# Short convolution and attention of a hybrid layer: two stages behind a barrier rewritten as one interleaved stage with other functions and another attention tail

## Chip, cores, metric

One Trainium2 chip, all 8 cores (two dies, cores 0 to 3 and 4 to 7), each with its own part of the tokens. The time is that of the slowest core in microseconds (us) of the device. A program on all cores has a slow state in some executions, in which one die shows a lower granted clock; only fast runs are compared unless the text says otherwise. Engines: PE multiplies matrices, DVE is the vector engine, ACT the scalar engine, POOL the GpSimd engine, SP issues transfers.

## The reference, cut to what matters

Two trunk layers. Each projects the input once, and two mixers read the result: grouped-query attention, and a gated delta scan whose inputs first go through a short convolution of width 3 with Silu and a norm per head. The two mixers do not depend on one another until their outputs are merged.

```python
def l2norm(x):
    xf = x.astype(jnp.float32)
    return xf * lax.rsqrt(jnp.sum(xf * xf, axis=-1, keepdims=True) + EPS)

def short_conv(x, w):                       # 1536 channels, width 3
    ...
    for j in range(1, CONV_W):
        y = y + xp[:, j:j + T] * w[j]
    return jax.nn.silu(y)

def block_attention(q, k, v):               # blocks of 128 queries, softmax in float32
    ...
        s = jnp.einsum('bkgqd,bkjd->bkgqj', qblk, k).astype(jnp.float32) * scale
        p = jax.nn.softmax(s, axis=-1).astype(v.dtype)
        return jnp.einsum('bkgqj,bkjd->bkgqd', p, v)

# in trunk_layer:
    qkv_d = short_conv(jnp.concatenate([q_d, k_d, v_d], axis=-1), conv_w)
    q_d = l2norm(q_d ...) * (DK ** -0.5);  k_d = l2norm(k_d ...)
    ...
    o_a = block_attention(q_use ..., k_all, v_all)
    o_f, S_f = delta_chunked(q_d, k_d, v_d, ...)     # and the same backwards
```

## The kernel before

Everything is recorded by small helpers (`mm`, `act`, `tt`, `stt`, `cp`, `recip`, `dma`), each with the list of what it reads and what it writes; the program derives its semaphores from these names. All matmuls therefore show one line number in the profile, all activations another, and the tile names tell them apart. Stage B, the convolution, works on blocks of 256 tokens (20 a core and layer), and a barrier (`P.fence()`) stands between it and the attention.

```python
for c in range(12):                                   # 12 x 3 DVE instructions of 128x256
    tsc("dve", CV[:, c, :], PRET[:, c, 0:TB], cw[:, 0, c:c + 1], ...)
    stt("dve", CV[:, c, :], PRET[:, c, 1:TB + 1], ...)
    stt("dve", CV[:, c, :], PRET[:, c, 2:TB + 2], ...)
for c in range(12):
    act(CV[:, c, :], CV[:, c, :], AF.Silu, ...)
for c in range(8):                                    # norms of q and k
    act(STB[0][:, :TB], CV[:, c, :], AF.Square, ...)
    mm(psb(0)[:, :TB], C("blk", True), STB[0][:, :TB], ...)
    act(STG[0][:, :TB], psb(0)[:, :TB], AF.Sqrt, ...)
    recip(STG[0][:, :TB], STG[0][:, :TB], ...)        # DVE
    stt("dve", CV[:, c, :], CV[:, c, :], ..., STG[0][:, :TB], ...)
    cp("act", STB[i][:, :TB], CV[:, c, :], ...)
    dma("pool", dstT..., STB[i][:, :TB], [f"stb{i}"], [("qkdt", s.name)])
# ... six groups of four f32 transposes, a copy and a transfer each
P.fence()
```

The attention runs over "items": one key tile of 128 against one block of 128 queries of 8 heads. The QK matmuls of item n+1 are recorded before the AV matmuls of item n (`LAG = 1`), with two score and two probability buffers. A block of the long sequence has 34 items, and ends with this tail:

```python
    for g in range(2): mm(PS[r_]..., KT_all..., QBz[qp][g], ...)      # QK of item idx
    act(XBW[r_], PS[r_], AF.Exp, ..., scale=0.125)                    # 128x1024
    for g in range(2): mm(psb(4 + g), VAp[:, kt, g, :], XBW[r_]...)   # AV of item idx - 1
    if last:
        for g in range(2):
            cp("dve", RS[64:65, :], psb(ob)[64:65, :], ...)           # the row of sums
            recip(RS[64:65, :], RS[64:65, :], ...)
            mm(psb(6)[0:64, :], C("ones")[64:65, 0:64], RS[64:65, :], ...)
            cp("dve", STG[0][0:64, :], psb(ob)[0:64, :], ...)
            tt("dve", OB, STG[0][0:64, :], psb(6)[0:64, :], ALU.mult, ...)
            dma("sp", OA..., OB..., ...)
```

## Time and profile before

| | before |
|---|---|
| time, median of 16 runs | 23658.64 us (23517.87 to 23765.41; the first four, which the prediction had, 23707.53) |
| stage B plus attention, per layer, by core | 3213 to 3265 us, mean 3235 |
| everything else of the span, by core | 17032 to 17233 us |
| loads of ACT's function tables in these stages, layer 0 | 41 |

The stage is measured on each core from the first load of the convolution's input (or of the context, if earlier) to the scan's first state load. The prediction shows the busy times and the costliest groups. For comparison with the same view after the change, here is the view of waits for the attention of layer 0 on core 4, the slowest core (columns: engine, output tile and line of what waited, what released it, then us in total, times, longest):

```profile
ACT sb_xbw L484 <- PE ps L478: 802.3, 591, 14.5
PE ps L478 <- DVE sb_bigB L505: 372.6, 80, 5.5
```

Such a wait is named after the last link of the chain, not after its cause: the first row contains the second, PE's own wait for the reciprocal of one row (line 505).

### The profile page before, as it was taken

The page shows a single profiled execution, that of the slowest core. Times are in us where ns is not written, and L with a number is a line of the kernel's source. Part 1 is how long each engine was busy: PE and PEld are TensorE (multiplying, and loading weights), DVE is VectorE, ACT ScalarE, POOL GpSimd, SP SyncE. Part 2 cuts the span into 40 slices and gives each one's busy share as a digit, 9 for nine tenths or more (in the row PEclk, how much of TensorE's full clock was granted, in tenths as well). Part 3 has the DMA queues.
Part 4 walks back from the last instruction along what each step waited for, and adds up shares of the span by engine and source line. Part 5 has one row for each costly group of instructions (what it writes and reads, how often), then busy time and mean ns, then how long its engine had stood idle before and what let it go on. Part 6 is the DMA issues. An engine that isn't in the chain of part 4 may idle for free.

```text
span 23694.1 us, 384038 instructions; the slowest of 8 cores (23508.7 to 23694.1 us)
## 1 busy us (share of the span) xinstructions
PE 12329.6 (52%) x116476; PEld 7884.9 (33%) x116700; DVE 8493.7 (36%) x13539; ACT 6954.8 (29%) x11204; POOL 4030.9 (17%) x5166
## 2 busy tenths in 40 slices
PE   2555115775655544574655521477566555349255
PEld 1333101222443333463533310122244333237144
DVE  0222452214666543220122245321365665322022
ACT  0444235663222221111134432466322222112011
POOL 1112110001333321110111211000033333111011
PEclk9777557886666667676777755687766666668577
DMA  5111110000011113311311111000011111332111
GB/s 122 47 46 44 46 48 14 5 5 18 28 29 30 30 38 91 89 67 47 85 55 47 46 44 48 22 5 5 13 28 29 30 27 29 84 95 77 28 41 39
DMA packets 1051188, 1018.80 MB, mean 43 GB/s; under 512 B 427456, under 2 KB 921024, under 8 KB 1038400
## 3 DMA queue, kind: packets, MB, share of 16 engines
q1 hardware_dynamic: 920576, 621.68, 9.2%
q0 software_dynamic: 128576, 372.53, 5.8%
q8 instruction: 967, 15.84, 0.3%
q14 instruction: 1069, 8.76, 0.1%
HBM read 688.84 MB, written 392.23 MB: 46 GB/s over the span
## 4 chain that ended last, share of the span: by engine, by line
PE 35%; DVE 18%; DMA 15%; ACT 13%; issue 13%; POOL 3%; POOLq 1%; ACTq 1%; SPq 0%; DVEq 0%
PE ps L478 34%; ACT sb_xbw L484 4%; DVE sb_stg L505 3%; DVE sb_bigB L487 3%; DMA gates_s<-sb_stb 3%; DVE sb_bigB L496 2%; DVE sb_bigB L505 2%; ACT L484 2%; DMA sb_warena<-w 2%; DMA pre_s<-sb_stg 1%; PE ps L481 1%; ACT sb_stb L484 1%; DVE sb_warena L487 1%; ACT sb_stg L484 1%; POOLq L184 1%
## 5 line engine op out<-in xcount | busy, mean ns | idle before, releaser
L478 PE MATMUL ps<-sb_hb,sb_warena 128*128 128x256 bf16 x18080 | 2538.2, 307 | 2207.2 <-DMA sb_warena<-w 1144.0
L478 PEld LDWEIGHTS ps<-sb_hb,sb_warena 128*128 128x128 bf16 x18080 | 1961.4, 110 | 2713.0 <-issue 2287.0
L484 ACT ACTIVATE sb_xbw<-ps 128x1024 bf16<-128x1024 f32 x2208 | 2199.1, 1023 | 1637.3 <-PE ps L478 1611.1
L478 PE MATMUL ps<-sb_gatb,sb_warena 128*128 128x256 bf16 (+1 forms) x18080 | 2164.6, 289 | 215.5 <-POOL sb_gatb L487 138.5
L478 PEld LDWEIGHTS ps<-sb_gatb,sb_warena 128*128 128x128 bf16 (+1 forms) x18080 | 1765.0, 111 | 589.4 <-issue 265.0
L478 PE MATMUL ps<-sb_xbw,sb_warena 128*128 128x512 bf16 x4326 | 1402.0, 406 | 374.4 <-ACT sb_xbw L484 346.7
L505 DVE RECIPROCAL sb_stg<-sb_stg 128x256 f32<-128x256 f32 x520 | 911.3, 1752 | 1765.0 <-ACT sb_stg L484 1765.0
L484 ACT ACTIVATE sb_stg<-ps,sb_b1f 128x256 f32<-128x256 f32 x1280 | 603.0, 474 | 3047.2 <-PE ps L478 2871.8
L478 PE MATMUL ps<-sb_warena,sb_kt_all 128*128 128x512 bf16 x4322 | 1419.7, 411 | 105.1 <-DMA sb_warena<-qa_p 72.8
L478 PE MATMUL ps<-sb_warena 64*64 64x64 bf16 (+1 forms) x25600 | 1113.8, 228 | 612.4 <-DMA sb_warena<-od_s 147.3
L478 PE MATMUL ps<-sb_stb,sb_cstb 128*128 128x256 bf16 x520 | 177.3, 341 | 2375.4 <-ACT sb_stb L484 2119.2
L502 DVE COPY sb_bigB<-ps 1x512 f32<-1x512 f32 (+1 forms) x180 | 134.7, 749 | 3013.7 <-PE ps L478 2747.1
L484 ACT ACT_TABLE_LOAD x745 | 955.8, 1283 | 698.0 <-PE ps L478 322.1
L478 PEld LDWEIGHTS ps<-sb_warena 64*64 64x64 bf16 (+1 forms) x25600 | 898.4, 129 | 782.6 <-issue 705.9
L487 POOL TENSOR_TENSOR sb_bigA<-sb_cst,sb_sm 128x512 f32<-128x512 f32 x160 | 163.3, 1042 | 5444.9 <-DMA sb_ktc<-kdt_s 3881.3
L487 DVE TENSOR_TENSOR sb_gatb<-sb_stg 128x256 bf16<-128x256 f32 x640 | 272.2, 425 | 2248.0 <-ACT sb_stg L484 2033.4
L487 POOL TENSOR_TENSOR sb_hb<-sb_hb,sb_cstb 128x512 bf16<-128x512 bf16 x560 | 659.2, 1195 | 1686.6 <-DVE sb_hb L487 1285.7
L478 PEld LDWEIGHTS ps<-sb_stb,sb_cstb 128*128 128x128 bf16 x520 | 52.6, 101 | 2514.7 <-issue 2514.6
L478 PEld LDWEIGHTS ps<-sb_xbw,sb_warena 128*128 128x128 bf16 x4416 | 311.0, 99 | 1366.5 <-issue 1356.2
L481 PE MATMUL ps<-sb_cst,sb_bigB 128*128 128x128 f32 x1440 | 372.3, 421 | 710.0 <-DVE sb_bigB L487 585.9
L487 DVE TENSOR_TENSOR sb_bigB<-sb_bigB,ps 64x512 f32<-64x512 f32 x640 | 436.9, 683 | 813.4 <-ACT sb_bigB L500 633.9
L478 PEld LDWEIGHTS ps<-sb_warena,sb_kt_all 128*128 128x128 bf16 x4416 | 442.2, 102 | 807.3 <-issue 425.7
(233 smaller groups left out, 21222.3 us busy)
## 6 DMA issues: line engine op xcount, KB each, us to landing
sb_bigA<-xres_s SPq DMA_DIRECT2D x64, 1024.0 KB, 5.9
sb_bigA<-pre_s SPq DMA_DIRECT2D x32, 1548.0 KB, 7.6
sb_bigB<-xres_s SPq DMA_DIRECT2D x48, 1024.0 KB, 6.0
pre_s<-sb_stg POOLq DMA_DIRECT2D x384, 128.0 KB, 2.1
gates_s<-sb_stb POOLq DMA_DIRECT2D x512, 64.0 KB, 1.8
sb_hb<-h_s SPq DMA_DIRECT2D x64, 512.0 KB, 4.2
sb_warena<-w_mod POOLq DMA_DIRECT2D x32, 768.0 KB, 6.9
xres_s<-sb_bigA POOLq DMA_DIRECT2D x24, 1024.0 KB, 5.3
```

The source lines that it names most:

```text
L184: eng.wait_ge(prod.sig_sem, prod.sig_val)
L478: P.add("pe", lambda e: e.matmul(out, lhsT, rhs, start=start, stop=stop, **kw), reads, writes)
L481: P.add("pe", lambda e: e.transpose(out, in_, ident), reads, writes)
L484: P.add("act", lambda e: e.activation(out, in_, func, **kw), reads, writes)
L487: P.add(eng, lambda e: e.tensor_tensor(out, in0, in1, op), reads, writes)
L496: P.add(eng, lambda e: e.scalar_tensor_tensor(out, in0, scalar, in1, op0, op1), reads, writes)
L502: P.add(eng, lambda e: e.tensor_copy(out, in_), reads, writes)
L505: P.add("dve", lambda e: e.reciprocal(out, in_), reads, writes)
```

## The change

The intent is to let ACT and PE work on attention items while DVE convolves, and to take DVE's reciprocals and ACT's table switches off the path. Both stages become generators; Silu and the inverse square root are written with exp and ln alone; the tail copies its accumulators out of PSUM at once and is finished during the next items. The diff, cut (the convolution loop and the transposes keep their instructions, apart from one PSUM bank, `psb(7)`, and all copies on DVE):

```diff
-                for c in range(12):
-                    act(CV[:, c, :], CV[:, c, :], AF.Silu, [("cv", c)], [("cv", c)])
+                    for c4 in range(3):
+                        SG = PRET[:, cs_, 0:TB]                  # over the convolution's input
+                        act(SG, CV[:, cs_, :], AF.Exp, ck + ["bigA"], ["bigA"], scale=-1.0)
+                        act(SG, SG, AF.Ln, ["bigA"], ["bigA"], bias=1.0)
+                        act(SG, SG, AF.Exp, ["bigA"], ["bigA"], scale=-1.0)
+                        tt("dve", CV[:, cs_, :], CV[:, cs_, :], SG, ALU.mult, ck + ["bigA"], ck)
+                        yield
-                    act(STG[0][:, :TB], psb(0)[:, :TB], AF.Sqrt, [pk(0)], ["stg0"], bias=EPS, scale=1.0)
-                    recip(STG[0][:, :TB], STG[0][:, :TB], ["stg0"], ["stg0"])
+                        act(STG[1][:, :], psb(7)[:, :], AF.Ln, [pk(7)], ["stg1"], bias=EPS, scale=1.0)
+                        act(STG[1][:, :], STG[1][:, :], AF.Exp, ["stg1"], ["stg1"], scale=-0.5)
 ... two channels at a time; the bf16 result is copied back by POOL; yield after each
-        P.fence()
 ...
+        def tail(s, q0):
+            for g in range(2):
+                cp("dve", RS2[64:65, g * 512:(g + 1) * 512], psb(4 + g)[64:65, :], [pk(4 + g)], ["rs"])
+                cp("dve", NUM[g][0:64, :], psb(4 + g)[0:64, :], [pk(4 + g)], [("num", g), f"stg{2 * g}"])
+            def inv():
+                act(RS2[64:65, :], RS2[64:65, :], AF.Ln, ["rs"], ["rs"])
+                act(RI[64:65, :], RS2[64:65, :], AF.Exp, ["rs"], ["ri"], scale=-1.0)
+            def out(g): ...        # one-row matmul in bf16, DVE product, transfer
+            return [inv, lambda: out(0), lambda: out(1)]
 ...
+                    if last:
+                        for fn in pend: fn()
+                        pend[:] = tail(s, q0)
+                    elif pend:
+                        pend.pop(0)()
 ...
+        gB_, gAt_ = genB(), genAttn()
+        while not (doneB and doneA):
+            ... next(gB_)                                        # one piece of stage B
+            for _ in range(3 + (1 if it_ % 4 == 3 else 0)):
+                ... next(gAt_)                                   # then 3.25 items on average
+            it_ += 1
```

## The prediction

> **What bounds the kernel now.** I first read the clocks of the cores: spans of 23509 to 23694 us, both dies alike, so one core (core 4, the slowest) stands for all. Then I looked for the two stages that the change touches, the short convolution ("B") and the attention, by the first transfer of each: the loads of the convolution's input begin at 2456.1 us, those of the attention's queries at 3742.5, and the scan's first state load is at 5668.9; in layer 1 the same marks are 13812, 15092 and 17060. The table of busy time in these four stretches of core 4 (columns: stretch and its length, busy us of PE, weight loads, DVE, ACT and POOL with counts, granted clock, DMA share, GB/s):
> ```profile
> 2456.00:3742.00 1286.00, 181.59 (x642) 107.83 (x642) 680.29 (x1083) 373.83 (x840) 161.84 (x281) 0.50 0.14 46
> 3742.00:5669.00 1927.00, 1298.54 (x4484) 393.42 (x4576) 431.82 (x321) 1089.96 (x1105) 4.81 (x1) 0.84 0.03 6
> 13812.00:15092.00 1280.00, 181.32 (x641) 107.60 (x641) 672.62 (x1082) 373.64 (x840) 153.86 (x281) 0.50 0.14 46
> 15092.00:17060.00 1968.00, 1369.60 (x4485) 404.34 (x4577) 439.79 (x323) 1111.72 (x1105) 12.68 (x2) 0.79 0.03 6
> ```
> The reader is to see two stages of opposite kind, one after the other behind a barrier. B is 53% DVE, 29% ACT and nearly no PE; the attention is PE and ACT with DVE idle. Together 3213 us in layer 0 and 3248 in layer 1: 6461 of 23694 us. No engine is full in either, so both are bound by waits. The groups by form say which, for B:
> ```profile
> L505 DVE RECIPROCAL sb_stg<-sb_stg 128x256 f32<-128x256 f32 x160 | 280.4, 1753 | 422.8 <-ACT sb_stg L484 422.8
> L496 DVE SCALAR_TENSOR_TENSOR sb_bigB<-sb_bigA,sb_cw,sb_bigB 128x256 f32<-128x256 f32 x480 | 232.5, 484 | 51.2 <-DVE sb_bigB L491 0.9
> L484 ACT ACT_TABLE_LOAD x40 | 51.3, 1283 | 32.5 <-DVE sb_bigB L496 19.8 <-PE ps L478 11.9 <-DVE sb_bigB L491 0.8
> ```
> and for the attention:
> ```profile
> L484 ACT ACTIVATE sb_xbw<-ps 128x1024 bf16<-128x1024 f32 x1103 | 1087.7, 1022 | 799.4 <-PE ps L478 788.5 <-ACT sb_xbw L484 1.6
> L505 DVE RECIPROCAL sb_bigB<-sb_bigB 1x512 f32<-1x512 f32 x77 | 257.5, 3344 | 8.6 <-DVE sb_bigB L502 0.9
> L478 PE MATMUL ps<-sb_bigB,sb_cst 1*64 1x512 f32 x152 | 146.0, 1061 | 354.3 <-DVE sb_bigB L505 354.3
> ```
> In B each of 160 normalisations goes round ACT, PE, ACT, DVE: the reciprocal alone is 1.753 us and DVE waits another 2.6 (422.8/160) for ACT. In the attention ACT waits 799 us for PE; half of that (354 us) is PE waiting for the 3.3 us reciprocal of a single row at the end of every query block. The order of time inside a query block shows the rest:
> ```profile
> 4306.37 1.94 ACT L484 ACTIVATE sb_xbw<-ps 128x1024 bf16<-128x1024 f32 x2 [0.40 <-PE ps L478]
> 4308.72 1.02 ACT L484 ACTIVATE sb_xbw<-ps 128x1024 bf16<-128x1024 f32 x1 [0.41 <-PE ps L478]
> ```
> Two exponentials (one "item" each: a key tile of 128) start every 4308.72 - 4306.37 = 2.35 us, so 1.172 us an item, ACT busy 1.94 of it: a ring of exp, AV, QK, exp with two score buffers. 34 items make 40 us; the next block starts 55 us after this one, so a tail costs 15 us.
>
> [...] stage B is at 0.50 throughout, after each tail 128x512 matmuls run 0.43 us apart for some 4 us and then 0.213, and in layer 1 there are dense stretches at about 0.77 to 0.81 in which two items take 2.53 us (1.265 each). [...] 1283 ns a load, none between exp and ln in the input projection, none between ln and a following square. [...] the trace has 1.02 us for 1024 columns, about 0.60 for 512, 0.41 for 256. [...] the trace shows a small DVE cast held for 7.73 us under POOL's memset. The new POOL copies (4 per block) are too few for this to matter.
>
> **The change, part by part.** (1) B and the attention become two generators, and the program takes one piece of B (17 per block of 256 tokens, 340 per layer) and then 3.25 attention items (1105 per layer); both run out together, without the barrier between. (2) Silu becomes exp(-ln(1+exp(-x))) on 1024 columns and a DVE product; square root and reciprocal become exp(-0.5 ln). All reciprocals on DVE are gone, and all ACT functions are of one table set. (3) The attention's tail copies sums and numerators out of PSUM (4 copies of 0.68 us) and leaves the inversion (ln, exp of one row on ACT) and the product for the next items; the one-row matmul becomes bf16.
>
> What a layer then costs, counted along ACT and the ring:
> - Items of the long sequence: 32 x 34 = 1088. The ring is 1.172 at full clock, 1.265 at 13/16; I choose 1.22: 1327 us.
> - Tails, 32. The next block's first AV waits for all four copies: AV 0.6, 4 x 0.69, then QK 0.6, and meanwhile ACT does two exponentials and ln and exp of 1024 columns (2 x 1.02). From the end of the last exponential to the third one of the next block I count 5.0 us in place of 2.35: 2.7 extra. DVE is sometimes in a convolution piece (3 x 1.44 us) when the copies come, and the two product matmuls sit in PE's order: 1.3 more, an estimate. 32 x 4 = 128 us (now 32 x 15 = 480).
> - Prompt sequences, 8 query blocks of 2 items: copies, ln, exp, two matmul-and-product pairs in a row, about 7 us each: 56 (now 183, from 5487 to 5670).
> - B on ACT per block: three sigmoid pieces of 3 x 1.04 + 0.2 = 3.3, and four normalisations of 3 x 0.60 + 0.6 (square to matmul to ln, the wait that now stands in the trace) + 0.1 = 2.5: 9.9 + 10.0 = 19.9. Each of these seven lets PE catch up and swallows part of the ring's 0.40 wait, 0.3 on average: -2.1.
> - B on PE per block: six groups of four f32 transposes, 0.87 us each put into the ring, some of it in slack: 6 x 0.7 = 4.2.
> - The sigmoid overwrites the convolution's input, so it waits for all twelve channels: 12 x 1.44 = 17.3 us on DVE against some 19 us of attention items; nearly even, 1 us per block.
> - Sum of B: 19.9 - 2.1 + 4.2 + 1 = 23 us x 20 blocks = 460.
> Together 1327 + 128 + 56 + 460 = 1971, and the 16 us of context loads and memset at the head stay: 1987 us a layer, for 3213 and 3248. Saved 1226 + 1261 = 2487; 23707 - 2487 = 21220. I say 21200.
> DVE: conv 17.3, products 3 x 1.2, scalings 4 x 0.8, copies 6 x 0.69 = 28 us a block, 565 in all, and tails 40 x 4.1 = 164: 730 of 1987. PE at full clock: 4416 x 0.213 + 20 x 6 + 20 = 1080. POOL: 14 transfers a block, each held for the landing of the one before (0.54 + 1.97 us in the trace), 35 us, and 4 copies of about 1 us: 39 of some 99 us. None of the three is the bound. ACT: 1104 x 0.97 + 20 x 17.2 + 40 x 2.04 = 1497, 75%.
>
> **The rivals.** (a) ACT alone sets the pace: with PE's work always done ahead the layer needs 1497 + 16 us, and the time is about 20250. For it: ACT gets 430 us more work, which hides the ring's wait. Against: the score buffers stay two and the order stays item by item, so ten of seventeen pieces bring ACT nothing and the ring's wait stays there. (b) The table sets are switched: were exp and ln not shared, 180 groups a layer would load twice, 180 x 2 x 1.283 = 462 us, so some 22100. Against: exp and ln back to back in the input projection. (c) The clock: always at 13/16 adds 49 us a layer (21320); at half clock four matmuls take 1.71 us, 1888 us an attention, some 22200. Against the last: the longest PE waits that I count are near 4 us at a tail, and B's matmuls fill in. (d) In-order queues couple: a sigmoid waiting for DVE stops the exponentials behind it, and an attention tail stops the convolution, each feeding the other; 5 us per block would add 200 us in all. (e) Nothing is gained because the two stages fight for ACT: the sums above exclude it, since the removed waits (DVE's 423, ACT's 799) are far more than the added ACT work.
>
> **Range and chances.** The sum rests on the ring's period (plus or minus 50 us a layer), the tails (40) and B's coupling (100); with half of (a) to one side and (c) and (d) to the other I put 8 in 10 on 20800 to 21600. Even (b) or the half clock leaves 6% of gain: faster 0.97, same 0.02, slower 0.01.
>
> **What would show it.** In the profile after: the stretch from the first query load to the scan at about 1990 us; ACT about three quarters busy in it and its largest wait still PE; one table load or a few in the stretch; PE's clock 0.8 to 1.0 with no stretch at 0.50 but the prompt blocks; about 4 us between the last exponential of a block and the third of the next beyond the ring; no DVE reciprocal. Wrong if ACT is over 85% busy (then (a)), if there are hundreds of loads (b), if the clock is at 0.5 to 0.6 (c), or if ACT waits mainly for DVE (d). The other stages should stay within 1%.

At the marks rules are cut that did not come from a trace or a run of this case. The 13/16 is the 0.8125 of the trace's own clock records (100 of the 1470 on core 4); half clock is their 0.50 and full clock their 1.

## The result and the profile after

The changed kernel took 21193.46 us (median of 11 runs, 20982.98 to 21290.18). Its time over that of the kernel before is 0.8945 (95% interval 0.8912 to 0.8977). This and all ratios below are the mean time of one kernel's fast runs over that of the other's fast runs of the same rounds, so not quite the ratio of the medians quoted. All outputs were correct, here and in every experiment.

The stage takes 1977 to 2034 us a layer on the eight cores (mean of both layers and all cores 1996); all else takes 17017 to 17199 us, as before. Core 1, the slowest (same columns as the first fence of the prediction), one line for the stage in each layer:

```profile
2455.00:4447.00 1992.00, 1369.18 (x5058) 467.30 (x5058) 676.69 (x1224) 1496.88 (x1604) 210.81 (x362) 0.86 0.12 35
12669.00:14658.00 1989.00, 1365.95 (x5057) 467.15 (x5057) 676.58 (x1224) 1496.84 (x1604) 206.41 (x362) 0.86 0.12 35
```

Two lines stand where four stood before. ACT is busy 1497 us of 1992, 75%, and DVE's 677 us lie beside it instead of alone. The groups by form in the stretch of layer 0 (busy us, mean ns, then idle time just before them and who ended it):

```profile
L484 ACT ACTIVATE sb_xbw<-ps 128x1024 bf16<-128x1024 f32 x1104 | 1098.3, 1021 | 367.4 <-PE ps L478 362.0 <-ACT sb_xbw L484 1.2
...
L484 ACT ACTIVATE sb_bigA<-sb_bigB 128x1024 f32<-128x1024 f32 x60 | 63.3, 1054 | 15.9 <-DVE sb_bigB L496 8.1 <-issue 7.6
...
L496 DVE SCALAR_TENSOR_TENSOR sb_stb<-sb_bigB,sb_stg 128x512 bf16<-128x512 f32 x80 | 55.4, 693 | 415.5 <-ACT sb_stg L484 415.5
```

The exponential costs what it cost, but waits 362 us for PE instead of 788.5 (in the prediction's window). The second row is the first pass of the sigmoid: in 60 pieces it waited only 8 us for the convolution. The third shows why idle time must be read with the bound in mind: DVE waits as long for ACT as it did before (415.5 against 422.8 us), and it no longer matters, because ACT is doing items meanwhile. There is no table load and no DVE reciprocal in the stretch. All of ACT's larger waits there:

```profile
ACT sb_xbw L484 <- PE ps L478: 362.0, 536, 27.5
ACT sb_stg L484 <- PE ps L478: 56.4, 79, 0.9
ACT sb_warena L484 <- DVE sb_warena L502: 26.1, 28, 5.4
ACT sb_bigA L484 <- DVE sb_bigB L496: 8.1, 7, 2.2
```

They add up to 453 us: the ring of score buffers, the norm's matmul, the tail's copies, the convolution. In order of time, ACT alone (start, us, operation, and in brackets the idle time before it):

```profile
2998.61 0.60 ACT L484 ACTIVATE sb_stg<-ps 128x512 f32<-128x512 f32 x1 [0.67 <-PE ps L478]
2999.30 0.63 ACT L484 ACTIVATE sb_stg<-sb_stg 128x512 f32<-128x512 f32 x1
2999.84 1.92 ACT L484 ACTIVATE sb_xbw<-ps 128x1024 bf16<-128x1024 f32 x2
3002.16 1.02 ACT L484 ACTIVATE sb_xbw<-ps 128x1024 bf16<-128x1024 f32 x1 [0.41 <-PE ps L478]
3003.68 2.20 ACT L484 ACTIVATE sb_warena<-sb_warena 1x1024 f32<-1x1024 f32 x2 [0.49 <-DVE sb_warena L502]
3005.89 0.63 ACT L484 ACTIVATE sb_stb<-sb_bigB 128x512 bf16<-128x512 f32 x1
```

A norm (two passes, no load between), two exponentials without a wait because PE had caught up during the norm, one with the ring's 0.41 us, then the tail's ln and exp in 2.20 us, and the next norm at once. A tail that was 15 us of idle is a step among others.

One thing in this trace was not foreseen. PE's granted clock (the third column from the end below) falls to half for short stretches inside the stage:

```profile
2880.00:2899.00 19.00, 14.57 (x33) 3.58 (x32) 5.93 (x8) 13.42 (x16) 1.09 (x2) 0.50 0.31 93
2899.00:2912.00 13.00, 7.76 (x32) 2.35 (x29) 1.38 (x2) 10.45 (x14) 3.25 (x6) 0.99 0.10 29
3036.00:3050.00 14.00, 12.03 (x50) 3.84 (x48) 11.79 (x28) 12.04 (x13) 0.54 (x1) 1.00 0.03 9
```

The first begins after a sigmoid piece, in which PE had nothing to do:

```profile
2876.28 2.21 ACT L484 ACTIVATE sb_bigA<-sb_bigA 128x1024 f32<-128x1024 f32 x2
2878.39 1.92 ACT L484 ACTIVATE sb_xbw<-ps 128x1024 bf16<-128x1024 f32 x2
...
2879.54 1.01 PE L478 MATMUL ps<-sb_xbw,sb_warena 128*128 128x512 bf16 x2 [3.07 <-ACT sb_xbw L484]
...
2881.56 1.02 ACT L484 ACTIVATE sb_xbw<-ps 128x1024 bf16<-128x1024 f32 x1 [1.25 <-PE ps L478]
```

PE waits 3.07 us for ACT, then runs at half clock, and the ring's wait grows from 0.33 or 0.41 to 1.25 us. Counted by the starts of successive attention matmuls in layer 0 of this core, 523 followed each other 0.40 to 0.45 us apart (before, core 4: 368). The trace also holds the records of the granted clock themselves. While the blocks of the long sequence run (2500 to 4350 us) they have 66 stretches at 0.50, together 416 us. Before the change (3760 to 5487 us on core 4) there were 32 stretches, together 423 us, one at each tail. So the time at half clock is about the same, but it now comes in twice as many pieces, and these lie among the items.

### The profile page after: what moved, and what is told of

Read it like the earlier page. It is cut to its first block, busy times and chain, and to the rows that moved or that the text cites. A ratio compares the mean times of both kernels' runs of the same rounds, so it can differ in the third digit from the quotient of the medians.

```text
span 21178.4 us, 380510 instructions; the slowest of 8 cores (21028.7 to 21178.4 us)
## 1 busy us (share of the span) xinstructions
PE 12029.8 (57%) x116380; PEld 7799.7 (37%) x116380; DVE 7624.0 (36%) x13179; ACT 7008.5 (33%) x10522; POOL 4116.3 (19%) x5326
## 4 chain that ended last, share of the span: by engine, by line
PE 38%; DMA 16%; ACT 14%; issue 13%; DVE 13%; POOL 3%; POOLq 1%; ACTq 1%; SPq 1%; DVEq 0%
PE ps L478 37%; ACT sb_xbw L484 4%; DVE sb_bigB L487 3%; DMA gates_s<-sb_stb 3%; ACT L484 2%; DMA sb_warena<-w 2%; DMA pre_s<-sb_stg 1%; DVE sb_bigB L496 1%; PE ps L481 1%; ACT sb_stb L484 1%; ACT sb_bigA L484 1%; DVE sb_warena L487 1%; POOLq L184 1%; DVE sb_stg L505 1%; ACT sb_hb L484 1%
## 5 line engine op out<-in xcount | busy, mean ns | idle before, releaser
L478 PE MATMUL ps<-sb_xbw,sb_warena 128*128 128x512 bf16 x4416 | 1503.6, 423 | 864.4 <-ACT sb_xbw L484 689.5
L478 PE MATMUL ps<-sb_warena,sb_kt_all 128*128 128x512 bf16 x4416 | 1487.9, 422 | 114.5 <-DMA sb_warena<-qa_s 49.7
L484 ACT ACTIVATE sb_stb<-ps 128x256 bf16<-128x256 f32 (+1 forms) x920 | 372.4, 405 | 1021.3 <-PE ps L478 454.6
L500 ACT CAST sb_sbf<-sb_bigB 64x512 bf16<-64x512 f32 x340 | 210.3, 619 | 1487.0 <-DVE sb_bigB L487 1219.7
L505 DVE RECIPROCAL sb_stg<-sb_stg 128x256 f32<-128x256 f32 x200 | 350.5, 1753 | 935.8 <-ACT sb_stg L484 935.6
L487 POOL TENSOR_TENSOR sb_warena<-sb_warena,sb_cstb 128x512 bf16<-128x512 bf16 x560 | 663.5, 1202 | 14.7 <-POOL sb_hb L487 11.1
L505 DVE RECIPROCAL sb_rstd<-sb_r 128x256 f32<-128x256 f32 x80 | 140.3, 1753 | 1404.2 <-ACT sb_r L484 1404.2
L478 PE MATMUL ps<-sb_bigA,sb_cst 128*128 128x512 f32 x480 | 383.5, 892 | 451.5 <-POOL sb_bigA L487 258.4
```

The source lines that it names most:

```text
L478: P.add("pe", lambda e: e.matmul(out, lhsT, rhs, start=start, stop=stop, **kw), reads, writes)
L484: P.add("act", lambda e: e.activation(out, in_, func, **kw), reads, writes)
L487: P.add(eng, lambda e: e.tensor_tensor(out, in0, in1, op), reads, writes)
L500: P.add("act", lambda e: e.copy(out, in_), reads, writes)
L505: P.add("dve", lambda e: e.reciprocal(out, in_), reads, writes)
```

## The experiments

Twelve kernels ran, in three calls, each call on one chip together with the kernel before (medians of 7 runs each: 23735.58, 23621.22 and 23623.92 us). The rest of the program, which no edit touches, took 16939 to 17393 us by core and execution, so stage durations are compared first and times second. The mean of the stage over both layers and eight cores, with the range:

| kernel | stage, us a layer | time, median us | ratio to before |
|---|---|---|---|
| before | 3235 (3213 to 3265) | 23658.64 | 1 |
| changed | 1996 (1977 to 2034) | 21193.46 | 0.8945 |
| changed, as a control later | 1983 (1975 to 1989) | 21318.04 | 0.9017 |
| not interleaved | 2849 (2803 to 2892) | 22959.84 | 0.9686 |
| not interleaved, own names | 2638 (2606 to 2678) | 22466.3 | 0.9518 |
| own names | 1989 (1975 to 2014) | 21292.94 | 0.9034 |
| tail alone | 2832 (2785 to 2882) | 22951.78, mostly slow | none used |
| old functions | 2206 (2194 to 2222) | 21803.04 | 0.9196 |
| old tail | 2430 (2401 to 2463) | 22195.63 | 0.937 |
| two items | 2076 (2067 to 2090) | 21462.01 | 0.9102 |
| own sigmoid buffer | 1953 (1938 to 1979) | 21122.1 | 0.8965 |
| QK ahead | 1864 (1854 to 1891) | 21026.51 | 0.8888 |
| two copies | 1976 (1961 to 2001) | 21080.08 | 0.8933 |
| all three edits | 1793 (1769 to 1834) | 20902.25 | 0.8854 |

My theory: the gain has three parts that need one another. The deferred tail takes some 9 to 11 us off each query block; the interleaving lets ACT's waits in B and in the ring fill each other; and the exp and ln forms are worth something only because, once interleaved, every function switch (1.283 us a load in the trace before) would land between two exponentials. Rivals: that the new functions alone make B short; that the tail alone carries the gain; that the overlap hides nothing because both stages want ACT.

### Everything but the interleaving

```diff
-        gB_, gAt_ = genB(), genAttn()
+        for _ in genB():
+            pass
+        P.fence()
+        gB_, gAt_ = iter(()), genAttn()
```

> All of the changed convolution stage first, then a barrier, then all of the changed attention: the interleaving alone is undone. My theory: the two removed waits (reciprocals) and the overlap give about half of the gain each. Attention alone 1327 + 128 + 56 + 16 = about 1530 us a layer; the convolution alone about 52 us a block (17.3 convolution, three sigmoid pieces 4, four normalisations 2.5 to 3, six transposes 2): 1050 a layer. Stage 2580 us a layer in place of 1990, so 21190 + 2 x 590 = about 22370 us. Rival (e), that the interleaving gives nothing because both stages want ACT: about 21200.

Measured: 22959.84 us (5 runs, ratio 0.9686, 0.9628 to 0.9745), 590 us more than I expected. The attention alone, from the first load of queries, took 1494 to 1582 us, 1543 on the mean of all cores (before 1926 to 1979, mean 1948), so there the new tail works. But B alone took 1305 us, 65 us a block, no less than the old B's 1287, though DVE is busy 515 us in it instead of 680, the norm rounds are half as many and no loads are left. So the interleaving is worth 2849 - 1996 = 853 us a layer, two thirds of the gain of 1239, and the length that I had expected of B was wrong. The waits of B on core 4 name two suspects:

```profile
ACT sb_bigA L484 <- DVE sb_bigB L496: 802.0, 20, 42.6
...
POOL qdt_s L475 <- DMA qdt_s<-sb_stb: 84.9, 39, 5.3
POOL kdt_s L475 <- DMA kdt_s<-sb_stb: 80.7, 46, 3.7
POOL vtm_s L475 <- DMA ktm_s<-sb_stb: 63.6, 31, 3.1
```

ACT stands idle 40 us a block until the convolution is done, of which the convolution itself takes 17. The other half lies before it, in the order of time:

```profile
3015.98 0.54 POOL L475 DMA_DIRECT2D qdt_s<-sb_stb  x1 [2.21 <-DMA qdt_s<-sb_stb]
3016.52 0.62 POOL L502 CAST sb_bigB<-sb_stb 128x512 f32<-128x512 bf16 x1
3017.98 0.69 DVE L502 CAST sb_stb<-ps 128x512 bf16<-128x512 f32 x1 [4.49 <-DMA qdt_s<-sb_stb]
3018.41 0.54 POOL L475 DMA_DIRECT2D kdt_s<-sb_stb  x1 [1.27 <-DMA qdt_s<-sb_stb]
```

POOL issues a transfer (0.54 us), waits for an earlier one to land (2.21 and 1.27 us here), issues the next; DVE waits 4.49 us for a buffer that a transfer still holds, and the copies back wait in POOL's queue behind the transfers. This is the program's own doing: all transfers of a kind are recorded as writes of one name, so each waits for the one before. The waits in the three rows above are 1.8 to 2.2 us on average, each after an issue of 0.54.

### The same, with a name of its own for each transfer

```diff
-  STB[i][:, k * TB:(k + 1) * TB], [f"stb{i}"], [("qkdt", s.name)])
+  STB[i][:, k * TB:(k + 1) * TB], [f"stb{i}"], [("qkdt", s.name, blk, c, k)])
-  dma("pool", dstM..., STB[i][:, :], [f"stb{i}"], [("tm", s.name)])
+  dma("pool", dstM..., STB[i][:, :], [f"stb{i}"], [("tm", s.name, blk, t2, grp)])
```

> The serial kernel (all of stage B with the new functions, a barrier, all of attention with the new tail; 22960 us, stage B 1305 us a layer, 65 us a block) in which the fourteen transfers of a block out of stage B no longer count as writes of one and the same tensor part, so that the queue that issues them does not wait for the landing of the transfer before. Theory: in the serial stage B it was this chain of landings (fourteen of about 2.5 us, 35 us a block) that the normalisations and transposes waited for, and my 52 us a block holds without it: stage B falls to about 1040 to 1100 us a layer, the whole to about 22500 us. Rival: the block is bound by its own chain over scalar, tensor and vector engine and the 17 us of convolution; then stage B stays above 1270 us a layer and the time within 70 us of 22960.

Measured: 22466.3 us (ratio 0.9518, 0.9471 to 0.9564), B 1113 us a layer, 55.6 a block. No wait of POOL for a landing is left in the stage. The same row of waits, for the serial kernel above 802.0, is now

```profile
ACT sb_bigA L484 <- DVE sb_bigB L496: 618.1, 20, 39.7
```

so this wait of ACT got 184 us shorter and B 192 us. In the old B of core 4, POOL's waits for landings add up to 166 us, against 360 in the serial kernel; its largest wait there is 402 us for ACT's copies. That the chain of landings became the longer one because there are half as many rounds of norms is my reading. The old B was not run with own names, so how much of 1287 - 1113 us is due to the new functions and how much to the names stays open. My expectation of B without the chain, 1040 to 1100 us, was nearly met.

### The changed kernel with these names

> The changed kernel (interleaved, 21193 us) with the same edit to the transfers out of stage B. In it a block of stage B has about 98 us and the chain of landings takes about 35 of them beside the items, so I expect no change: within 40 us of the changed kernel, a stage of 1970 to 2030 us. If it gets faster by over 80 us, the landings also delay the interleaved stage, by way of the buffers that the transfers hold or the shared normalisation buffers.

Measured: 21292.94 us (ratio 0.9034, 0.8992 to 0.9076), stage 1975 to 2014 us against 1977 to 2034. No gain: a block has about 100 us when interleaved, and the chain of landings lies beside the items. The same chain costs some 200 us a layer in one schedule and nothing in the other. So of the 853 us that the interleaving is worth, some 200 are the hiding of this chain: with own names in both kernels it is worth 2638 - 1989 = 649 us a layer.

### The tail alone

The old stage B and barrier, with the new tail in the attention.

```diff
-                if last:
-                    for g in range(2): ... recip ... mm ... cp ... tt ... dma
+                if last:
+                    for fn in pend: fn()
+                    pend[:] = tail(s, q0)
+                elif pend:
+                    pend.pop(0)()
```

> The kernel before with the new attention tail alone (deferred inversion on ACT, sums copied out of PSUM first). Theory: a tail of a long query block falls from 15 us to about 4, 32 x 11 = 350 us a layer, and the prompt blocks from 183 to about 60: together some 470 us a layer, so 23660 - 940 = about 22720 us. A rival in which the tail is hidden anyway: 23660.

Measured: 22951.78 us as the median of 4 runs, of which three are slow; the only fast run took 22707.65. The profile is of a slow run too, so its stage of 2832 us compares slow with fast. Its attention, 1497 to 1596 us and 1546 on the mean, is that of the serial kernel (1543), whose profile is of a fast run; from fast profiles alone the new tail is thus worth 1948 - 1543 = 405 us a layer. What a tail adds to the plain interval between two exponentials fell from 13.8 us (15.02 - 1.24) to 4.8 (3.2 for ln and exp, 0.78 for each one-row matmul), 40 times 9.0 = 360 us, and the plain interval itself from 1.236 to 1.175 us. By the stage of this run it is 3235 - 2832 = 403 us a layer. The serial kernel, with the new functions on top, has the same stage (2849), so serially these functions gave nothing as long as the landings held B up.

### Interleaved, with the old functions

```diff
-   act(SG, CV[:, cs_, :], AF.Exp, ...); act(SG, SG, AF.Ln, ...); act(SG, SG, AF.Exp, ...); tt("dve", ...)
+   act(CV[:, cs_, :], CV[:, cs_, :], AF.Silu, ck, ck)
-   act(STG[1][:, :], psb(7)[:, :], AF.Ln, ...); act(STG[1][:, :], STG[1][:, :], AF.Exp, ..., scale=-0.5)
+   act(STG[1][:, :], psb(7)[:, :], AF.Sqrt, ...); recip(STG[1][:, :], STG[1][:, :], ["stg1"], ["stg1"])
```

> The changed kernel with silu, square root and the DVE reciprocal in the interleaved convolution, in place of exp and ln. Theory: every sigmoid piece and every normalisation now leaves the table of the attention's exp and comes back: 14 loads a block, 280 a layer (560 in all) at 1.283 us, 359 us a layer; against it ACT saves six passes of 1.06 us and four of 0.6 a block, 8.8 x 20 = 175 us. Net +185 us a layer: about 21560 us. If the loads were hidden behind waits (a rival): about 20850, faster than the changed kernel.

Measured: 21803.04 us (ratio 0.9196, 0.9129 to 0.9264), stage 2206 us, 210 us a layer more than the changed kernel where I expected 185. The time missed by 240 us, 50 of them by the stage. In the profiled execution the rest of the program also ran longer on one die (17351 to 17393 us); the control of the changed kernel shows as much (17336 to 17393) with no edit at all. The groups of the stage on core 0:

```profile
L484 ACT ACT_TABLE_LOAD x280 | 359.2, 1283 | 67.5 <-PE ps L478 64.5
L505 DVE RECIPROCAL sb_stg<-sb_stg 128x512 f32<-128x512 f32 x80 | 268.2, 3353 | 673.5 <-ACT sb_stg L484 673.5
```

280 loads, two for each of the 140 groups: a norm between two exponentials now takes 5.54 us, 2.02 more than with ln and exp. Two loads are 2.57 us, and the exp pass that falls away gives back 0.54: 2.03. The 3.35 us reciprocals lie beside and cost nothing. A sigmoid piece took only 0.20 us more, since one Silu and two loads (1.06 + 2.57) replace three passes (3.3).

### Interleaved, with the old tail

> The changed kernel with the old attention tail (two reciprocals of a row on DVE, with PE waiting for each). Theory: PE's order stops for about 14 us per tail and ACT soon with it, minus what ACT gets from the convolution: about 9 us more per long block (32) and 14 per prompt block (8): 400 us a layer, about 22000 us. Rival: the interleaved convolution fills the hole, and the time stays at 21200.

The edit puts the old tail's lines, as shown for the kernel before, into the new attention generator. Measured: 22195.63 us (ratio 0.937, 0.9314 to 0.9427), stage 2430 us, 434 a layer above the changed kernel (expected 400). The stage on core 0:

```profile
L505 DVE RECIPROCAL sb_warena<-sb_warena 1x512 f32<-1x512 f32 x80 | 267.5, 3344 | 8.6 <-DVE sb_warena L502 0.5
...
L478 PE MATMUL ps<-sb_warena,sb_cst 1*64 1x512 f32 x160 | 153.2, 1058 | 391.2 <-DVE sb_warena L505 391.2
```

PE waits 391 us for the one-row reciprocals, as it did before, and every engine behind PE with it. Interleaving did not hide this wait, which stands in the queue of the engine that the items need.

### Fewer items between the pieces

```diff
-            for _ in range(3 + (1 if it_ % 4 == 3 else 0)):
+            for _ in range(2):
```

> The changed kernel with two attention items between two pieces of stage B instead of 3.25, the rest as changed. So the 340 pieces are spread over 680 of the 1105 items, and the last 424 items run alone. Theory of the feeding: the convolution of a block is about 17 us on the vector engine, and until its first sigmoid step the scalar engine has only the items laid between; with 3.25 items there are about 13 of them (16 us of ring at 1.25 us), which just covers it; with 2 there are 8 (10 us), so the scalar engine waits some 7 us a block, 20 blocks, 2 layers: about 280 us more, 21590 us against 21318 in the earlier control of the changed kernel, and the waits of the attention exponential or of the sigmoid steps for the vector engine's convolution grow by some 130 us a layer. Rival: only the sum of the work counts and the order is free, then the time stays within 40 us of the changed kernel's.

Measured: 21462.01 us (ratio 0.9102, 0.9057 to 0.9147), stage 2076 us, 80 us a layer more; I had expected 140. ACT now waits for the convolution in every block:

```profile
ACT sb_bigA L484 <- DVE sb_bigB L496: 73.2, 20, 4.6
ACT sb_warena L484 <- DVE sb_warena L502: 69.6, 40, 5.5
```

20 waits of 3.7 us instead of 8 us in all, and 43 us more for the tail's copies, which queue behind the convolution on DVE. The direction holds, and by the stage the rival (only the sum of work counts) falls; the wait for the convolution is half of what I reckoned.

### A buffer of its own for the sigmoid

```diff
-                        SG = PRET[:, cs_, 0:TB]
-                        act(SG, CV[:, cs_, :], AF.Exp, ck + ["bigA"], ["bigA"], scale=-1.0)
+                        SG = SGB[c4 % 2]
+                        act(SG, CV[:, cs_, :], AF.Exp, ck, [("sg", c4 % 2)], scale=-1.0)
```

> The changed kernel with a buffer of its own (two in turn) for the sigmoid steps, which so far are written over the input of the convolution and therefore wait until all twelve channels are convolved. Nothing else is changed. If the wait for the whole convolution is hidden by the items between, it is worth at most about 1 us a block, 20 to 40 us in all (about 21160 to 21180 against 21193 of the changed kernel). If what made the kernel with all three edits faster than the one with the probability buffer alone (1772 against 1860 us a stage on the cores with the higher clock) is this buffer, it is worth 50 to 80 us a stage, 100 to 160 us in all (about 21050 us), and the scalar engine's waits in the stage fall by that.

Measured: 21122.1 us (ratio 0.8965, 0.8921 to 0.9008), stage 1953 us, 43 a layer less than the changed kernel's 1996 and 30 less than the control's 1983, although only 8 us of wait stood against it. ACT's wait for the convolution is gone (8 us), and its wait for PE fell from 362 to 329 us on the core that I read (core 4): the plain intervals between exponentials get 1.215 us long instead of 1.251. That the sigmoid pieces wander earlier is my explanation, not shown. Neither of my two figures (10 to 20 us a layer, or 50 to 80) was right; the effect lies between. The times can't separate it from the changed kernel (0.8945 in its own rounds).

### QK one item further ahead

```diff
-        LAG = 1
+        LAG = 2
+        XP = [XBW[0], XBW[1], WAR[:, 15872:16896]]
```

(with the three probability buffers used in turn). This kernel, the next and the kernel with all edits ran together with the changed kernel as a control.

> The changed kernel itself, as the control on the same chip as the three that follow: about 21200 us.

Measured: 21318.04 us (ratio 0.9017), stage 1975 to 1989 us: the stage repeats, the rest was longer in these executions.

> The changed kernel with the scores' matmul of an item put two items ahead of its value matmul in PE's order, and a third buffer for the probabilities (the score buffers stay two). Theory: the ring is exp, AV, QK, exp, 2.35 us for two items; with QK ahead of AV it is exp, QK, exp, about 1.85 us, below ACT's own 1.94 to 2.02 for two, so ACT sets the pace and most of its 362 us of waits for PE in the stage go: 270 us a layer, about 20650 us. If PE's clock falls to 13/16 in the denser stage, four matmuls take 1.05 us and some of it is lost: 20800. Rival: the wait is not the order's but the score buffers' or PE's throughput; then about 21200.

Measured: 21026.51 us (6 runs, three of them fast; ratio 0.8888, 0.8809 to 0.8967), stage 1864 us, 119 a layer less than the control where I expected 270. ACT's waits on core 4, from a profiled run that fell in the slow state, though the stage there is as long as on the other die:

```profile
ACT sb_xbw L484 <- PE ps L478: 165.5, 161, 25.7
ACT sb_stg L484 <- PE ps L478: 62.2, 80, 1.2
ACT sb_warena L484 <- PE ps L478: 57.6, 82, 9.7
ACT sb_bigA L484 <- DVE sb_bigB L496: 34.0, 14, 4.9
```

The exponentials (of the third buffer in the third row) wait 223 us instead of 362, and faster items leave the convolution less time, so that wait grows from 8 to 34 us. Sorted by the records of the granted clock, 58 of the 223 us fall at 0.50, 44 at full clock, 16 across a change, and 105 are nine waits of over 5 us, six of them in the prompt blocks. The same sorting of the changed kernel's 362 gives 124, 157, 30 and 50. So the edit took away most of the waits at full clock, half of those at half clock, and made the prompt blocks' longer. Two stretches of different clock:

```profile
3038.00:3048.00 10.00, 8.93 (x20) 2.43 (x21) 3.58 (x5) 8.76 (x9) 0.00 (x0) 0.50 0.04 7
3048.00:3058.00 10.00, 5.78 (x25) 1.94 (x23) 1.23 (x1) 9.36 (x11) 0.00 (x0) 0.99 0.04 7
```

At half clock PE is busy 8.93 of 10 us, with ACT not far behind (8.76, a sigmoid piece and a tail among it); at full clock ACT is busy 9.36 and PE 5.78. A plain interval, with nothing but items in it, lasts 0.948 us at full clock (640 of them) and 1.436 at 0.50 (72). My expectation had assumed full clock everywhere.

### Two copies instead of four in the tail

The sums lie in row 64 just below the numerators, so one copy of 65 rows replaces two.

```diff
-  cp("dve", RS2[64:65, ...], psb(4 + g)[64:65, :], ...)
-  cp("dve", NUM[g][0:64, :], psb(4 + g)[0:64, :], ...)
+  cp("dve", NUM[g][0:65, :], psb(4 + g)[0:65, :], ...)
```

> The changed kernel with two copies in place of four at the attention's tail (numerators and sums in one copy of 65 rows). Theory: the next block's second value matmul waits 1.4 us less, in 40 tails a layer, and ACT pays 0.2 us more for two logarithms: 1.2 x 80 = 96 us, about 21100 us. Rival: the wait at the tail is set by ACT's inversion and not by the copies: 21200.

Measured: 21080.08 us (ratio 0.8933, 0.8857 to 0.901). The time came out as expected, but not for the expected reason: the stage, 1976 us, is 7 us shorter than in the control, not 48. The rest of the executions was shorter. This edit is not shown to be worth anything by itself.

### All three edits

> QK ahead, two copies, and a buffer of its own for the sigmoid, so that it no longer waits for the whole convolution of its block. Theory: the sum of the two above and 20 to 40 us for the sigmoid's wait: about 20520 us (20350 to 20750).

Measured: 20902.25 us (20853.15 to 20912.91, 4 runs, ratio 0.8854, 0.8801 to 0.8907), stage 1793 us, 190 a layer less than the control, which is more than the three edits gave one by one (119 + 7 + 30), and yet 380 us of time short of what I expected. It beats both kernels, the changed kernel of the same rounds by 1.8% only (0.8854 / 0.9017 = 0.982; the intervals do not overlap). The waits of ACT on core 4 go some way to say why: beside the QK ahead alone, the sigmoid's wait for the convolution (34 us there, 8 in the changed kernel) is gone, that for the tail's copies fell from 33 to 15 us, and that for PE from 223 to 180. What sets the stage now can be seen between two cores of one execution, core 0 and core 4:

```profile
2500.00:4200.00 1700.00, 1334.24 (x4944) 511.45 (x4943) 578.07 (x1082) 1461.83 (x1600) 193.54 (x357) 0.81 0.13 39
```

```profile
2500.00:4200.00 1700.00, 1255.98 (x4869) 478.51 (x4967) 586.68 (x1095) 1445.96 (x1609) 196.17 (x360) 0.88 0.13 39
```

With a granted clock of 0.81 the stage is 1829 us, with 0.88 it is 1773. On the core with the low clock 1855 of the attention's matmuls were 0.235 to 0.30 us apart in layer 0, on the other 206. So between these two cores PE's clock counts for 56 us a layer now, next to ACT's 1500.

## Why the prediction was right

The time (21200 for 21193), the stage (1987 for 1977 to 2034) and ACT's busy time (1497 for 1497) came out, the time's closeness in part by luck. To see whether the terms did too, all intervals between successive attention exponentials of core 1, layer 0 were sorted by what else ACT or PE did in them (means; "extra" is beyond the plain interval of 1.251 us):

| term | predicted | measured |
|---|---|---|
| item of the ring | 1.22 us | 1.251 us mean, 1.149 median |
| norm of two channels, extra | 2.5 - 0.3 = 2.2 us | 2.27 us |
| sigmoid of four channels, extra | 3.3 - 0.3 + 1/3 = 3.3 us | 3.25 us |
| group of transposes, extra | 0.7 us | 0.23 us; 120 of them: -56 us |
| tail, extra | 4 us, 7 in the prompts: 184 us | 3.0 for ln and exp, 0.75 for each one-row matmul: 4.5 us, 180 us |
| items and tails together | 1327 + 184 = 1511 us | 1104 x 1.251 + 180 = 1561: +50 us |
| head and end | 16 us | 25.6 + 19.2 us: +29 us |

With 80 x 2.27 = 182 for the norms, 60 x 3.25 = 195 for the sigmoids and 28 for the transposes the measured terms sum to 2011, 19 more than the stage, since steps that fall between the same two exponentials share their extra. So the sum was right partly because errors happened to meet: transposes were over-sized by 56 us (most of them lie in PE's slack), the ring and its tails under-sized by 50, the ends by 29.

Step by step:
- What bounded the kernel: right. Both stages were waits; serial B stays as long with a quarter of its DVE work taken away and gets 192 us shorter when its transfers no longer wait for one another, and the attention gives up some 400 us with the tail alone.
- The deferred tail: right, and shown twice, 403 us a layer serially, 434 interleaved; by the prediction's own terms 480 + 183 - 184 = 479, so its size was put some 50 to 75 us too high.
- One table set: right. No load is in the stage after, and putting the old functions back costs about 210 us. Rival (b) reckoned 462 for loads in all 180 groups; 140 groups load twice (280 loads in that run), and each saves a pass.
- Interleaving: right in sum, and shown to be worth 853 us a layer by the serial kernel, 649 without the chain of landings. Rival (e), a fight for ACT, falls with it. The parts overlap: undone one at a time they cost 853, 210 and 434 us, more than the whole gain of 1239.
- Rival (a), ACT alone sets the pace: wrong, as said. With the QK further ahead the stage came down by 119 of the 453 us of waits, with all edits by 190.
- Rival (d), coupling by queues: there, but small: 8 us of waits for the convolution and 26 for the tail's copies a layer. Two items between pieces bring it out. The record has one more coupling that I had passed over: two of ACT's waits, 11.5 and 11.3 us in layer 0, come from a query block whose load SP issued only after the convolution's next input (at 3173.38 and 3169.34 us for the first), so that PE waited 10.09 us for it.
- The clock: this check failed. "No stretch at 0.50 but the prompt blocks" is not so: outside the head and the prompt blocks there are 66 short ones, 416 us in layer 0. The step that failed is the one that looked only at the waits of near 4 us at a tail. That waits of this length are the ones that matter was an estimate from the trace before, where PE waits 4.17 and 5.17 us for the reciprocals of a tail and the matmuls after it run 0.43 us apart. The records come in steps of 3.41 us. Before the change (core 4) each of the 32 falls to 0.50 had a pause of PE of at least that length that reached into the 7 us before it; after it (core 1) 44 of 65 had none. In the step before each of the 65, PE was idle 2.31 us in the median, and all the time in only nine (these counts are estimates, since the ends of matmuls are modelled). What makes the clock fall is not shown. Sorted by the records, the plain intervals take 1.144 us at full clock (589 of them), 1.254 at 0.8125 (48), 1.972 at 0.50 (74) and 1.423 across a change (58): 83 us more over the 769 plain intervals than all at full clock, before the change some 31 (core 4). This is a sorting, not an experiment: no run took the half clock away with everything else unchanged, and an interval can be long for another reason and fall at 0.50 as well. My 1.22 had been chosen as a middle between the 1.172 seen at full clock and the 1.265 seen at 0.77 to 0.81, and so was near the mean by luck.

What stays open: why the sigmoid's own buffer also shortens ACT's waits for PE; how much of the three edits' surplus over their sum the waits named above explain; what normalising two channels at a time is worth, which every run of the new stage has and none undoes; and why the rest of the program differs by some 400 us between fast executions.

## What to carry to other kernels

When two independent stages are each bound by waits, recording them alternately can be worth more than speeding up either: here it was worth 853 us a layer, and a quarter of stage B's vector work was saved for nothing while it stood alone and its transfers waited for one another. Before interleaving, clear what would stop the engine that both need (a one-row reciprocal of 3.344 us in PE's path, a function switch of two loads of 1.283 us between exponentials), since interleaving did not hide these here: put back, they cost 434 and 210 us a layer. Count such a change along the engine that will be busiest, interval by interval, and check the terms afterwards and not only the sum; and look at the records for chains that a shorter stage will expose, such as transfers that wait for one another because they share a name.
